# Fixed issue orders around the first experts, and scattered rows read back through slots of the weight ring

## The chip, the cores and the metric

The kernel runs on one core of a Trainium2 chip. The metric is the device time of one execution in microseconds; less is better. The profile is one execution of the same program, with every instruction and every DMA packet recorded. Its engines are PE (matmuls; PEld is the weight load in front of them), DVE (element-wise work), ACT (activations and copies), POOL (small work and indirect DMAs) and SP (a queue that issues DMAs).

## The reference

One transformer layer on 512 tokens of width 1024, in float32: a mixer of three branches (short convolution, sparse attention, gated delta rule), and behind it a hierarchical mixture of experts. The change touches only the second half:

```python
def hier_moe(h, w_rg, b_rg, w_re, b_re, w_eg, w_eu, w_ed):
    ...                               # a group of 4, then 2 of its 8 experts, per token
    order = jnp.argsort(expert)       # tokens sorted by expert
    ...
    def expert_block(args):
        xb, e = args
        return (jax.nn.silu(xb @ w_eg[e]) * (xb @ w_eu[e])) @ w_ed[e]
    ...
    return jax.ops.segment_sum(y, tok_s, num_segments=n_tok).reshape(b, s, dm)
```

There are 32 experts. Each has a gate and an up matrix of 1024x512 and a down matrix of 512x1024, and each of the 512 tokens goes to two experts.

## The kernel before

**Order of work.** The program is traced in Python, and a scheduler then puts each engine's instructions into an order of its own, by the order of the trace and by when it believes their inputs to be there. An engine works through its queue strictly in that order: an instruction that waits holds up all behind it. Two calls add edges. `tc.issue_after(ins)` puts what a block traces on the engine of `ins` behind `ins` in that queue, and does not wait for its end. `tc.keep_in_program_order(ins)` puts one instruction behind the one traced before it on the same engine.

**Experts in pairs.** After the router (L951 to L1007) each expert has 64 slots for tokens. Experts `e` and `e + 16` form a pair, so that there are 16 pairs, and the loop at L1276 runs over them. For each pair the 128 slots' token rows are gathered (`xg`), turned by eight transposes on PE (`pxg`) and scaled on DVE into `xT` (L1109). For each expert of the pair `ffn_up` runs 32 matmuls into `pgu` (L1166, L1167), ACT applies Silu (L1177), DVE multiplies by the up half (L1178), PE turns the result (`pt`, L1184), DVE copies it out as `aT` (L1185), and `ffn_down` runs 16 matmuls into `pd` (L1208).

**Two ways back.** For the pairs in `by_rows` (0, 1, 2, 4, 6, 8, 10) ACT copies `pd` out as `yd`, and POOL scatters its rows by an indirect DMA into `yrows` in DRAM (L1217). For the other pairs the result is split into a high and a low part `y` (L1199 on ACT, L1200 on DVE), DVE makes a 0/1 matrix `sel` from the tokens' numbers `toks` (L1193), and PE multiplies the two into `pc` (L1256), which DVE adds to the output rows `x1p` (L1258). `add_rows` (L1228), called in pairs 12 and 13, works out the row numbers `rix` on POOL, zeroes a tile `yr` for each half of a token tile (L1240), gathers the scattered rows into it (L1241), and has DVE add it to `x1p` (L1245). That is eight `yr` tiles of 128x1024.

**Tables.** The router's results are scattered into eight tables in DRAM, `islots` (L1051), read back into `itab` (L1082), and added up on POOL (L1085, L1086) into `info`. From that POOL makes `tix` (which rows to gather), `yix` (where to scatter), `toks` and `rg` (scales), L1089 to L1101. Pairs 0 and 1 do not need them all: pair 0's rows are picked by matmuls (L1122), and `first_info` (L1132) makes `tix0` for pair 1 and the scales of both.

**Buffers.** The gathered `xg` and the `yr` tiles share one tag of two buffers (`ringa`, tag `raw`). The weights come in chunks of 1 MB through a ring of 18 slots, 12 chunks to a pair, in the order of L1288 and L1290; `wchunk` (L1065) takes the next slot and SP issues the load (L1071), which waits until the slot's last user is done.

```python
    def wchunk(shape, src):
        pool, tag = slots[nslot[0] % len(slots)]
        nslot[0] += 1
        w = pool.tile(shape, F32, tag=tag, name="we")
        ...
            nc.sync.dma_start(w, src)
```

The last expert's down weights come in three pieces, each with its matmuls (L1328), sums and stores.

Of the kernel before, what the change touches and what calls it, by code (L numbers as in the profile page):

```python
# [27 lines left out]
NEXP = 32  # L28
# [71 lines left out]
def kernel(ctx, tc, x, w_in, w_nat, w_small, w_gate, w_branch, w_out, cmp_w1, cmp_w2,  # L100
                       w_rt, consts, params, norm, w_eg, w_eu, w_ed, out, dbg=None):
    nc = tc.nc
    V, A, T, G = nc.vector, nc.scalar, nc.tensor, nc.gpsimd
# [273 lines left out]
    for c in range(NT):  # L377
# [31 lines left out]
        for h in range(4):  # L409
            i = 4 * c + h  # L410
# [609 lines left out]
    b4 = lambda ap, n: ap.unsqueeze(2).to_broadcast([P, NT, n])  # L1020
    V.tensor_tensor(out=ex, in0=ex, in1=mg.to_broadcast([P, NT, 4]), op=ALU.subtract)
    V.tensor_tensor(out=exs[:, :, 4:5], in0=m2, in1=m1, op=ALU.subtract)
    A.activation(exs, exs, AF.Exp)
    A.activation(sc[:, 63:64], mhalf, AF.Silu)
    V.tensor_reduce(out=se, in_=ex, axis=AX.X, op=ALU.add)
    V.scalar_tensor_tensor(out=den, in0=e2, scalar=1.0, in1=se, op0=ALU.add, op1=ALU.mult)
    V.reciprocal(den, den)
# [52 lines left out]
    itab = pair_input().rearrange("p k s -> p (k s)")[:, 0:512].rearrange("p (j c) -> p j c", c=64)  # L1080
    for j, tab in enumerate(islots):
        (nc.scalar if j < 4 else G).dma_start(itab[:, j], tab.rearrange("(p e) c -> p (e c)", p=P))  # L1082
    info = mp.tile([P, NEXP // 2, 4], F32, name="info")
    for n in (4, 2):
        G.tensor_tensor(out=itab[:, 0:n], in0=itab[:, 0:n], in1=itab[:, n:2 * n], op=ALU.add)  # L1085
    G.tensor_tensor(out=info.rearrange("p e c -> p (e c)"), in0=itab[:, 0], in1=itab[:, 1], op=ALU.add)  # L1086

    tix = mp.tile([P, NEXP // 2], I32, name="tix")
    G.tensor_scalar(out=tix, in0=info[:, :, 0], scalar1=4096.0, scalar2=None, op0=ALU.add)  # L1089


    toks, rg = (mp.tile([P, 2, NEXP // 2], F32, name=n) for n in ("toks", "rg"))
    yix = mp.tile([P, 2, NEXP // 2], I32, name="yix")
    for h in range(2):
        hs = slice(64 * h, 64 * h + 64)
        G.tensor_copy(rg[0:64, h], info[hs, :, 1])
        G.tensor_copy(rg[64:128, h], info[hs, :, 2])
        for a in range(2):
            G.tensor_scalar(out=yix[64 * a:64 * a + 64, h], in0=info[hs, :, 3], scalar1=2.0, scalar2=8192.0 + a,
                            op0=ALU.mult, op1=ALU.add)  # L1100
            G.tensor_scalar(out=toks[64 * a:64 * a + 64, h], in0=info[hs, :, 0], scalar1=4096.0, scalar2=None, op0=ALU.add)  # L1101

    def turned(xg):
        xT = pair_input()
# [27 lines left out]
    def first_info():  # L1132
        pi = ps_e.tile([P, 2, 4], F32, tag="pt", name="pi")
        for b in range(2):
            for t in range(NT):
                T.matmul(pi[:, b], row2(t, b), tg[:, t, b], start=t == 0, stop=t == NT - 1)
        V.tensor_copy(info0, pi)
        V.tensor_scalar(out=tix0, in0=info0[:, 1, 0:1], scalar1=4096.0, scalar2=None, op0=ALU.add)
        for h in range(2):
            V.tensor_copy(rg0[0:64, h], info0[64 * h:64 * h + 64, :, 1])  # L1140
            V.tensor_copy(rg0[64:128, h], info0[64 * h:64 * h + 64, :, 2 + h])


    def next_input(pair):
        xg = ringa.tile([P, D], F32, tag="raw", name="xg", bufs=2)
        if pair == 1:
            G.memset(xg, 0.0)
        idx = tix[:, pair:pair + 1] if pair > 1 else tix0
        G.indirect_dma_start(out=xg, out_offset=None, in_=x1rows, in_offset=bass.IndirectOffsetOnAxis(ap=idx, axis=0),
                             bounds_check=S - 1, oob_is_err=False)  # L1150
        inputs.append(turned(xg))

    def slot_info(src, hs):
        gsl = ep.tile([P, 1], F32, tag="gsl", name="gsl", bufs=2)
# [35 lines left out]
    def selection(tok):  # L1190
        sel = lp.tile([P, 512], F32R, tag=("fa", "fb")[nsel[0] % 2], name="sel")
        nsel[0] += 1
        V.tensor_scalar(out=sel, in0=iota, scalar1=tok, scalar2=None, op0=ALU.is_equal)  # L1193
        return sel


# [5 lines left out]
    def ffn_down(aT, wd, tok, between=None, to=None):  # L1202
        pd = mpsum("pd")

        def products(ks):
            for k in ks:
                for a in range(2):
                    T.matmul(pd[64 * a:64 * a + 64], aT[:, k], wd(k, a), start=k == 0, stop=k == 3)  # L1208
                combine_step()

        products((0, 1))
        with tc.issue_after(between()) if between else ExitStack():
            products((2, 3))
        if to is not None:
            y = ep.tile([P, D], F32, tag="y", name="yd", bufs=2)[:, 0:512]
            A.copy(out=y, in_=pd)
            G.indirect_dma_start(out=yrows, out_offset=bass.IndirectOffsetOnAxis(ap=to, axis=0), in_=y, in_offset=None,  # L1217
                                 bounds_check=4 * S - 1, oob_is_err=False)
            return
        y = ep.tile([P, D], F32R, tag="y", name="y", bufs=2)  # L1220
        for a in range(2):
            y_parts(y, halves[a], pd, a)
        rows.append((selection(tok), y))

    by_rows = (0, 1, 2, 4, 6, 8, 10)


    def add_rows(first, last):  # L1228
        if first == 0:
            G.memset(half, 8192.0)  # L1230
            for pair in by_rows:
                G.tensor_scalar(out=psl, in0=at_e, scalar1=float(pair), scalar2=-4096.0, op0=ALU.is_equal, op1=ALU.mult)
                G.tensor_tensor(out=half, in0=half, in1=psl, op=ALU.add)
            G.tensor_tensor(out=half, in0=half, in1=over, op=ALU.add)
            G.tensor_tensor(out=half, in0=half, in1=inf[:, :, :, 3], op=ALU.add)
            G.tensor_copy(rix, half)
        for n in range(first, last):
            t, i = n // 2, n % 2
            yr = ringa.tile([P, D], F32, tag="raw", name="yr", bufs=2)
            G.memset(yr, 0.0)  # L1240
            G.indirect_dma_start(out=yr, out_offset=None, in_=yrows.rearrange("(r a) n -> r (a n)", a=2),  # L1241
                                 in_offset=bass.IndirectOffsetOnAxis(ap=rix[:, t, i:i + 1], axis=0),
                                 bounds_check=2 * S - 1, oob_is_err=False)
            x1 = x1p[t // 2][:, t % 2]
            V.tensor_tensor(out=x1, in0=yr, in1=x1, op=ALU.add)  # L1245

    def combine(pieces=halves):
        todo.extend((tuple(rows), t, cols) for t in range(NT) for cols in pieces)
# [27 lines left out]
    for pair in range(NEXP // 2):  # L1276
# [12 lines left out]
        for h in range(1 if pair == NEXP // 2 - 1 else 2):  # L1289
            ffn_down(up[h][1], weights_down(w_ed[pair + 16 * h]), toks[:, h, pair:pair + 1],  # L1290
                     None if h else up[1][0], yix[:, h, pair:pair + 1] if pair in by_rows else None)
            if h == 0 and len(inputs) == pair + 1 < NEXP // 2:
                next_input(pair + 1)
            if h == 0 and pair in (12, 13):
                add_rows(4 * (pair - 12), 4 * (pair - 11))
        if len(rows) == 2:
            combine()
            rows.clear()
# [146 lines left out]
```

## Time and profile before

| | |
|---|---|
| median of 3 runs | 1226.16 us (1225.51 to 1228.13) |
| the profiled execution's own time | 1225.41 us |
| its span, first to last instruction | 1223.7 us |
| mean granted PE clock | 0.965 of full speed |
| PE busy | 1112.4 us (91%) |
| DVE busy | 555.2 us (45%) |
| ACT busy | 331.7 us (27%) |
| POOL busy | 126.5 us (10%) |
| moved by DMA | 272.42 MB, mean 223 GB/s |

The experts begin about 700 us after the span's start and fill the rest. Busy time of PE is modelled from pipelined matmuls, so that 91% says that PE seldom stands still and not that it runs at its peak. In rows of the timeline the columns are start, duration (both in us), engine, line, operation, output <- inputs, shapes, count, and in brackets how long the engine was idle before and what ended that. A line of the windows gives a stretch, its length, the busy time of PE, PEld, DVE, ACT and POOL with their instructions, and at the end the granted PE clock, the DMA engines' busy share and the rate in GB/s. Line numbers are those of the kernel before.

### The profile page before, as it was taken

To read this page: it belongs to the slowest core of one execution; us is meant where nothing else is said; L and a number is where in the kernel's file an instruction comes from. 1 tells how busy PE (TensorE), PEld (TensorE's weight loads), DVE (VectorE), ACT (ScalarE), POOL (GpSimd) and SP (SyncE) were. 2 spreads that over 40 slices of the span, in tenths; PEclk is the share of its full clock that TensorE was granted. 3 is DMA by queue.
4 is the path that set the end of the run, shared out by engine and by line. 5 is a ranking of instruction groups with operands and counts; after the bars stand their busy time and mean duration, and the time that the engine had idled before them with its cause. 6 is when DMAs were issued, how large, how long until landed. Compare 5 with 4: busy or idle time off the path is not lost.

```text
span 1223.7 us, 15803 instructions
## 1 busy us (share of the span) xinstructions
PE 1112.4 (91%) x6135; PEld 709.6 (58%) x6136; DVE 555.2 (45%) x1258; ACT 331.7 (27%) x644; POOL 126.5 (10%) x210
## 2 busy tenths in 40 slices
PE   0899999999999999999999969997899897997596
PEld 0788798987788887766899524332233333332233
DVE  1677576596444865565353611113041313143435
ACT  2444243343332635565233100110011010110011
POOL 3100211310010000000000341100000000001300
PEclk9999999999999999999999979999899999998799
DMA  8232234212223221100792589999999999999831
GB/s 326 60 101 86 87 94 147 71 52 87 70 71 95 87 86 54 51 2 19 285 376 120 188 322 372 421 420 419 420 420 419 422 420 419 421 420 419 349 137 71
DMA packets 53183, 272.42 MB, mean 223 GB/s; under 512 B 8715, under 2 KB 12683, under 8 KB 28272
## 3 DMA queue, kind: packets, MB, share of 16 engines
q1 hardware_dynamic: 44928, 254.95, 53.7%
q0 software_dynamic: 5600, 12.09, 2.6%
q10 hardware_dynamic: 2576, 4.32, 1.0%
q8 instruction: 50, 0.82, 0.3%
q14 instruction: 29, 0.24, 0.1%
HBM read 267.25 MB, written 12.34 MB: 228 GB/s over the span
## 4 chain that ended last, share of the span: by engine, by line
PE 76%; DMA 12%; issue 6%; DVE 2%; POOL 2%; ACT 1%; POOLq 0%; DVEq 0%; ACTq 0%
PE pgu L1166 9%; PE pmm L189 8%; PE pmm L187 8%; PE pmm L188 8%; PE pd L1208 7%; PE pgu L1167 5%; DMA we<-in_w_eu_dram 3%; PE po L831 3%; PE ptp L825 2%; DMA yr<-yrows,rix 2%; PE pb L188 2%; PE pb L187 2%; PE pb L189 2%; DMA yrows<-zero 2%; DMA we<-in_w_eg_dram 2%
## 5 line engine op out<-in xcount | busy, mean ns | idle before, releaser
L1166 PE MATMUL pgu<-we,xT 128*64 128x512 f32 x512 | 239.8, 615 | 26.4 <-DMA we<-in_w_eg_dram 24.0
L1167 PE MATMUL pgu<-we,xT 128*64 128x512 f32 x512 | 236.4, 608 | 1.4 <-DMA we<-in_w_eu_dram 1.4
L189 PE MATMUL pmm<-hTh,lo 128*128 128x512 f32 x432 | 171.9, 398 | 0.2 <-DVE lo L182 0.2
L187 PE MATMUL pmm<-hTh,hi 128*128 128x512 f32 x432 | 171.1, 396 | 0.0
L188 PE MATMUL pmm<-hTl,hi 128*128 128x512 f32 x432 | 170.7, 395 | 0.0
L182 DVE TENSOR_TENSOR lo<-raw,hi 128x1024 fp32r<-128x1024 f32 x82 | 100.4, 1224 | 114.9 <-ACT hi L181 112.6
L1166 PEld LDWEIGHTS pgu<-we,xT 128*64 128x64 f32 x512 | 68.2, 141 | 126.1 <-issue 117.2
L1208 PE MATMUL pd<-we,aT 128*64 128x512 f32 x496 | 128.4, 622 | 8.8 <-DVE aT L1185 8.8
L181 ACT CAST hi<-raw 128x1024 fp32r<-128x1024 f32 x82 | 86.1, 1050 | 163.9 <-PE pmm L188 94.5
L1177 ACT ACTIVATE act<-pgu,rg 64x512 f32<-64x512 f32 x32 | 21.8, 682 | 272.2 <-PE pgu L1167 182.0
L1167 PEld LDWEIGHTS pgu<-we,xT 128*64 128x64 f32 x512 | 67.2, 140 | 46.3 <-issue 39.4
L189 PEld LDWEIGHTS pmm<-hTh,lo 128*128 128x128 f32 x432 | 81.5, 189 | 17.8 <-DVE lo L182 1.8
L187 PEld LDWEIGHTS pmm<-hTh,hi 128*128 128x128 f32 x432 | 81.7, 189 | 16.6 <-DVE fa L704 0.6
L188 PEld LDWEIGHTS pmm<-hTl,hi 128*128 128x128 f32 x432 | 81.6, 189 | 16.5
L1208 PEld LDWEIGHTS pd<-we,aT 128*64 128x64 f32 x496 | 37.1, 141 | 70.8 <-issue 58.1
L1178 DVE SCALAR_TENSOR_TENSOR act<-pgu,rg,act 64x512 f32<-64x512 f32 x32 | 24.2, 756 | 116.5 <-ACT act L1177 116.1
L1258 DVE TENSOR_TENSOR x<-pc,x 128x512 f32<-128x512 f32 (+2 forms) x76 | 46.9, 658 | 33.2 <-PE pc L1256 32.8
L1185 DVE COPY aT<-pt 128x256 f32<-128x256 f32 x32 | 13.5, 423 | 101.0 <-PE pt L1184 96.9
L1256 PE MATMUL pc<-y,sel 128*128 128x512 f32 (+2 forms) x152 | 50.5, 440 | 8.1 <-DVE y L1200 5.1
L1256 PEld LDWEIGHTS pc<-y,sel 128*128 128x128 f32 x152 | 25.4, 194 | 45.2 <-issue 16.7
L1199 ACT CAST y<-pd 64x512 fp32r<-64x512 f32 (+2 forms) x40 | 21.2, 538 | 105.1 <-PE pd L1208 47.2
L1109 DVE TENSOR_TENSOR xT<-pxg,prm 128x512 f32<-128x512 f32 x32 | 20.9, 684 | 58.3 <-PE pxg L1108 54.7
(796 smaller groups left out, 1786.0 us busy)
## 6 DMA issues: line engine op xcount, KB each, us to landing
we<-in_w_eg_dram SPq DMA_DIRECT2D x64, 1024.0 KB, 20.1
we<-in_w_eu_dram SPq DMA_DIRECT2D x64, 1024.0 KB, 20.1
we<-in_w_ed_dram SPq DMA_DIRECT2D x62, 1024.0 KB, 19.9
raw<-in_w_in_dram SPq DMA_DIRECT2D x30, 512.0 KB, 3.5
raw<-in_w_gate_dram SPq DMA_DIRECT2D x24, 512.0 KB, 3.5
raw<-in_w_branch_dram SPq DMA_DIRECT2D x12, 512.0 KB, 3.5
yrows<-zero POOLq DMA_DIRECT2D x1, 4096.0 KB, 21.7
raw<-in_w_nat_dram SPq DMA_DIRECT2D x8, 512.0 KB, 3.6
```

Source lines behind the costliest of these rows:

```text
L181: A.copy(out=hi, in_=raw)
L182: V.tensor_tensor(out=lo, in0=raw, in1=hi.bitcast(F32), op=ALU.subtract)
L187: T.matmul(ps, ahi(k), bhi(k), start=start and k == 0, stop=False)
L188: T.matmul(ps, ahi(k), blo(k), start=False, stop=False)
L189: T.matmul(ps, alo(k), bhi(k), start=False, stop=stop and k == n - 1)
L825: T.transpose(ptp[:, kt * P:(kt + 1) * P], pts[i][:, kt * P:(kt + 1) * P], ident)
L831: T.matmul(po[64 * hh:64 * hh + 64, qs], nkv[:, kt, 256 + 128 * br + 64 * g:256 + 128 * br + 64 * g + 64], pT[hh][:, kt * P:(kt + 1) * P], ...
L1166: T.matmul(pgu[0:64], xs(k), wg(k), start=k == 0, stop=k == KT - 1)
L1167: ins = T.matmul(pgu[64:128], xs(k), wu(k), start=k == 0, stop=k == KT - 1)
L1208: T.matmul(pd[64 * a:64 * a + 64], aT[:, k], wd(k, a), start=k == 0, stop=k == 3)
L1256: T.matmul(pc[:, 0:n], sel[:, t * P:(t + 1) * P], y[:, cols], start=i == 0, stop=i == len(src) - 1)
L1258: V.tensor_tensor(out=xo, in0=pc[:, 0:n], in1=xo, op=ALU.add)
```

## The change

- The Silu activation of one dummy element (L1024), which loads ACT's table for Silu, is put behind the Exp of the router (L1023) in ACT's queue.
- The gather of pair 1's rows is issued inside `first_info`. The additions of the tables and what follows from them (L1084 to L1101) become a function `tables`, with the same instructions, and are put behind that gather in POOL's queue.
- Each `sel` is put behind the DVE instruction traced before it.
- `add_rows` works on a whole token tile per call: it is called four times instead of twice. The row numbers are worked out behind the last scatter in POOL's queue. Each `yr` is 128x2x1024 and takes a slot of the weights' ring instead of a buffer of `xg`. Its zeroing and its two gathers are put behind the last gather of `xg` traced by then. The DVE additions are still eight of 128x1024.

```diff
-    A.activation(exs, exs, AF.Exp)
-    A.activation(sc[:, 63:64], mhalf, AF.Silu)
+    with tc.issue_after(A.activation(exs, exs, AF.Exp).ins):
+        A.activation(sc[:, 63:64], mhalf, AF.Silu)
...
+    def tables():
+        for n in (4, 2):
+            G.tensor_tensor(out=itab[:, 0:n], in0=itab[:, 0:n], in1=itab[:, n:2 * n], op=ALU.add)
...
             V.tensor_copy(rg0[64:128, h], info0[64 * h:64 * h + 64, :, 2 + h])
-
-
-    def next_input(pair):
+        gathered.append(gather(1))
+        with tc.issue_after(gathered[0][1]):
+            tables()
+
+    gathered = []
+
+
+    def gather(pair):
         xg = ringa.tile([P, D], F32, tag="raw", name="xg", bufs=2)
         if pair == 1:
             G.memset(xg, 0.0)
         idx = tix[:, pair:pair + 1] if pair > 1 else tix0
...
+        return xg, ins.ins
+
+    def next_input(pair):
+        if pair > 1:
+            gathered.append(gather(pair))
+        inputs.append(turned(gathered[-1][0]))
...
-        V.tensor_scalar(out=sel, in0=iota, scalar1=tok, scalar2=None, op0=ALU.is_equal)
+        tc.keep_in_program_order(V.tensor_scalar(out=sel, in0=iota, scalar1=tok, scalar2=None, op0=ALU.is_equal))
...
+            last_scatter.append(ins.ins)
...
-    def add_rows(first, last):
-        if first == 0:
-            G.memset(half, 8192.0)
...
+    def add_rows(t):
+        if t == 0:
+            with tc.issue_after(last_scatter[-1]):
+                G.memset(half, 8192.0)
...
-        for n in range(first, last):
-            t, i = n // 2, n % 2
-            yr = ringa.tile([P, D], F32, tag="raw", name="yr", bufs=2)
+        pool, tag = slots[nslot[0] % len(slots)]
+        nslot[0] += 1
+        yr = pool.tile([P, 2, D], F32, tag=tag, name="yr")
+        with tc.issue_after(gathered[-1][1]):
             G.memset(yr, 0.0)
-            G.indirect_dma_start(out=yr, out_offset=None, in_=yrows.rearrange("(r a) n -> r (a n)", a=2),
...
-            x1 = x1p[t // 2][:, t % 2]
-            V.tensor_tensor(out=x1, in0=yr, in1=x1, op=ALU.add)
+            for i in range(2):
+                G.indirect_dma_start(out=yr[:, i], out_offset=None, in_=yrows.rearrange("(r a) n -> r (a n)", a=2),
...
+        x1 = x1p[t // 2][:, t % 2]
+        for i in range(2):
+            V.tensor_tensor(out=x1, in0=yr[:, i], in1=x1, op=ALU.add)
...
-            if h == 0 and pair in (12, 13):
-                add_rows(4 * (pair - 12), 4 * (pair - 11))
+            if pair in (12, 13):
+                add_rows(2 * (pair - 12) + h)
```

More of the change, by code (lines that the diff above doesn't have):

```diff
@@ L1083 @@
     info = mp.tile([P, NEXP // 2, 4], F32, name="info")
-    for n in (4, 2):
-        G.tensor_tensor(out=itab[:, 0:n], in0=itab[:, 0:n], in1=itab[:, n:2 * n], op=ALU.add)
-    G.tensor_tensor(out=info.rearrange("p e c -> p (e c)"), in0=itab[:, 0], in1=itab[:, 1], op=ALU.add)
     tix = mp.tile([P, NEXP // 2], I32, name="tix")
-    G.tensor_scalar(out=tix, in0=info[:, :, 0], scalar1=4096.0, scalar2=None, op0=ALU.add)
     toks, rg = (mp.tile([P, 2, NEXP // 2], F32, name=n) for n in ("toks", "rg"))
     yix = mp.tile([P, 2, NEXP // 2], I32, name="yix")
[L1094 to L1101, printed above, removed]
+    def tables():
+        for n in (4, 2):
+            G.tensor_tensor(out=itab[:, 0:n], in0=itab[:, 0:n], in1=itab[:, n:2 * n], op=ALU.add)
+        G.tensor_tensor(out=info.rearrange("p e c -> p (e c)"), in0=itab[:, 0], in1=itab[:, 1], op=ALU.add)
+        G.tensor_scalar(out=tix, in0=info[:, :, 0], scalar1=4096.0, scalar2=None, op0=ALU.add)
+        for h in range(2):
+            hs = slice(64 * h, 64 * h + 64)
+            G.tensor_copy(rg[0:64, h], info[hs, :, 1])
+            G.tensor_copy(rg[64:128, h], info[hs, :, 2])
+            for a in range(2):
+                G.tensor_scalar(out=yix[64 * a:64 * a + 64, h], in0=info[hs, :, 3], scalar1=2.0, scalar2=8192.0 + a,
+                                op0=ALU.mult, op1=ALU.add)
+                G.tensor_scalar(out=toks[64 * a:64 * a + 64, h], in0=info[hs, :, 0], scalar1=4096.0, scalar2=None, op0=ALU.add)
     def turned(xg):
@@ L1148, in next_input @@
         idx = tix[:, pair:pair + 1] if pair > 1 else tix0
-        G.indirect_dma_start(out=xg, out_offset=None, in_=x1rows, in_offset=bass.IndirectOffsetOnAxis(ap=idx, axis=0),
-                             bounds_check=S - 1, oob_is_err=False)
-        inputs.append(turned(xg))
+        ins = G.indirect_dma_start(out=xg, out_offset=None, in_=x1rows, in_offset=bass.IndirectOffsetOnAxis(ap=idx, axis=0),
+                                   bounds_check=S - 1, oob_is_err=False)
+        return xg, ins.ins
[3 more added lines that the diff above has]
+        inputs.append(turned(gathered[-1][0]))
     def slot_info(src, hs):
@@ L1216, in ffn_down @@
             A.copy(out=y, in_=pd)
-            G.indirect_dma_start(out=yrows, out_offset=bass.IndirectOffsetOnAxis(ap=to, axis=0), in_=y, in_offset=None,
-                                 bounds_check=4 * S - 1, oob_is_err=False)
+            ins = G.indirect_dma_start(out=yrows, out_offset=bass.IndirectOffsetOnAxis(ap=to, axis=0), in_=y, in_offset=None,
+                                       bounds_check=4 * S - 1, oob_is_err=False)
+            last_scatter.append(ins.ins)
             return
@@ L1225 @@
     by_rows = (0, 1, 2, 4, 6, 8, 10)
-    def add_rows(first, last):
-        if first == 0:
-            G.memset(half, 8192.0)
[L1231 to L1236, printed above, removed]
-        for n in range(first, last):
-            t, i = n // 2, n % 2
-            yr = ringa.tile([P, D], F32, tag="raw", name="yr", bufs=2)
[L1240 to L1243, printed above, removed]
-            x1 = x1p[t // 2][:, t % 2]
-            V.tensor_tensor(out=x1, in0=yr, in1=x1, op=ALU.add)
+    last_scatter = []
@@ new lines, in add_rows @@
+    def add_rows(t):
+        if t == 0:
+            with tc.issue_after(last_scatter[-1]):
+                G.memset(half, 8192.0)
+                for pair in by_rows:
+                    G.tensor_scalar(out=psl, in0=at_e, scalar1=float(pair), scalar2=-4096.0, op0=ALU.is_equal, op1=ALU.mult)
+                    G.tensor_tensor(out=half, in0=half, in1=psl, op=ALU.add)
+                G.tensor_tensor(out=half, in0=half, in1=over, op=ALU.add)
+                G.tensor_tensor(out=half, in0=half, in1=inf[:, :, :, 3], op=ALU.add)
+                G.tensor_copy(rix, half)
+        pool, tag = slots[nslot[0] % len(slots)]
+        nslot[0] += 1
+        yr = pool.tile([P, 2, D], F32, tag=tag, name="yr")
+        with tc.issue_after(gathered[-1][1]):
+            G.memset(yr, 0.0)
+            for i in range(2):
+                G.indirect_dma_start(out=yr[:, i], out_offset=None, in_=yrows.rearrange("(r a) n -> r (a n)", a=2),
+                                     in_offset=bass.IndirectOffsetOnAxis(ap=rix[:, t, i:i + 1], axis=0),
+                                     bounds_check=2 * S - 1, oob_is_err=False)
+        x1 = x1p[t // 2][:, t % 2]
+        for i in range(2):
+            V.tensor_tensor(out=x1, in0=yr[:, i], in1=x1, op=ALU.add)
```

## The prediction

> **What bounds the kernel now.** I read the page for the span, then the windows by stage, then the waits of PE, and at the two places where these show a hole, the timelines of DVE, PE, POOL and SP.
>
> ```profile
> span 1223.7 us, 15803 instructions
> ```
>
> ```profile
> we<-in_w_eg_dram SPq DMA_DIRECT2D x64, 1024.0 KB, 20.1
> ```
>
> ```profile
> 700.00:724.00 24.00, 15.21 (x76) 6.42 (x74) 2.55 (x9) 2.65 (x3) 14.57 (x35) 0.88 0.94 353
> 724.00:740.00 16.00, 13.27 (x46) 4.36 (x44) 2.90 (x5) 1.17 (x2) 4.14 (x9) 0.65 0.62 216
> 740.00:1130.00 390.00, 351.56 (x1543) 131.31 (x1540) 98.29 (x158) 38.20 (x62) 31.78 (x32) 0.95 1.01 418
> 1130.00:1146.00 16.00, 1.41 (x5) 0.71 (x5) 7.83 (x11) 2.22 (x4) 3.81 (x3) 0.50 1.00 414
> 1146.00:1175.00 29.00, 28.83 (x117) 10.82 (x117) 15.28 (x21) 1.36 (x2) 7.75 (x7) 0.96 0.83 312
> 1175.00:1210.00 35.00, 33.47 (x166) 13.44 (x162) 14.93 (x33) 5.66 (x11) 0.00 (x0) 1.00 0.00 0
> ```
>
> ```profile
> PE pgu L1166 <- DMA we<-in_w_eg_dram: 24.0, 4, 10.1
> PE pxg L1108 <- DMA xg<-x1rows,tix: 14.8, 2, 14.6
> PE pd L1208 <- DVE aT L1185: 8.8, 1, 8.8
> ```
>
> From 740 to 1130 the DMA engines are full (share 1.01, 418 GB/s): the weights set the pace, and PE waits for them 24.0 us in four places. A chunk (1024 KB, 1.05 MB) takes 2.5 us at that rate and lands 20.1 us after its issue, so eight are in flight and the ring's other ten slots hold landed chunks. Before 740 the DMA has a hole (0.62), because slots come free late. From 1130 to 1146 PE stands still for a gather, and after 1146 PE is full and the DMA runs dry (0.83, then 0.00): there PE sets the end.
>
> **The front: `sel`, the tables, the second gather.**
>
> ```profile
> 722.60 0.49 DVE L1193 TENSOR_SCALAR sel<-c_moe,toks 128x512 fp32r<-128x512 f32 x1 [10.15 <-POOL toks L1101]
> 723.11 0.42 DVE L1185 COPY aT<-pt 128x256 f32<-128x256 f32 x1
> 728.16 0.49 DVE L1193 TENSOR_SCALAR sel<-c_moe,toks 128x512 fp32r<-128x512 f32 x1 [4.62 <-POOL toks L1101]
> ```
>
> ```profile
> 714.35 0.46 PE L1184 MATMUL pt<-c_ident,act 64*128 64x64 f32 x4
> 723.59 3.68 PE L1208 MATMUL pd<-we,aT 128*64 128x512 f32 x8 [8.79 <-DVE aT L1185]
> 729.58 0.66 PE L1184 MATMUL pt<-c_ident,act 64*128 64x64 f32 x4 [2.31 <-DVE act L1178]
> 730.17 7.92 PE L1208 MATMUL pd<-we,aT 128*64 128x512 f32 x24
> ```
>
> ```profile
> 1081.86 3.65 PE L1208 MATMUL pd<-we,aT 128*64 128x512 f32 x16
> ```
>
> ```profile
> 727.32 0.33 SPq L1071 DMA_DIRECT2D we<-in_w_eg_dram  x1
> ```
>
> Two `sel` stand in DVE's queue at pair 0, which is in `by_rows` and uses none: they belong to pair 3 and wait for `toks`. Behind the first stands `aT` of expert 0, whose input PE had ready at 714.35 + 0.46 = 714.8; behind the second, the act of expert 1, for which PE waits 2.31. PE therefore ends pair 0 at 738.1, 23.3 us after 714.8. At the full clock 32 products at 3.65/16 = 0.23 are 7.3, the copy to `aT` 0.4 and the second turn 0.5, so 723 would do. And the chunk issued at 727.32 waited for the first down slot of pair 0. Pinned behind its own pair's `y`, `sel` waits for nothing here.
>
> What could be late next is pair 1's gather, and the tables.
>
> ```profile
> 717.43 0.72 POOL L1085 TENSOR_TENSOR xT<-xT 128x256 f32<-128x256 f32 x1 [1.71 <-DMA xT<-islots]
> ```
>
> ```profile
> 718.45 1.14 POOL L1149 DMA_INDIRECT xg<-x1rows,tix  x1 [0.16 <-issue]
> ```
>
> ```profile
> xg<-x1rows,tix POOLq DMA_INDIRECT x15, 8.6
> ```
>
> The gather stands behind a table sum that waits for `islots`; POOL was idle for the 1.71 us before it. In front of the sums the gather leaves by 715.7 at the latest and lands 8.6 us later, at 724.3 or before, about when PE wants it (723). Queued behind it on POOL are the sums, which start with their data at 717.4 in either order, and behind them pair 0's scatter and pair 2's gather, which PE wants one pair later: nothing added.
>
> What the front is worth is read from the DMA, since the DMA sets the pace up to 1130: 16 us at 0.62 leave 0.38 x 16 = 6.1 us idle. The 0.06 x 24 = 1.4 us before that are the wait for pair 0's first slot, which does not move. Bounds: 0, if other slots stay late; by rate instead of share 16 x (1 - 216/418) = 7.7. I take **-6.1**, the row that counts the engines' time.
>
> ```profile
> 709.68 1.28 ACT L1177 ACT_TABLE_LOAD   x1 [14.67 <-DMA xT<-islots]
> ```
>
> Silu behind Exp: this load goes from in front of expert 0's act into ACT's idle 14.67 us. The act comes earlier, but PE turns it only at 714.35, behind expert 1's matmuls: 0, at most -1.3.
>
> `sel` later elsewhere: 18 instructions of 0.49. At worst `pc` waits one `sel` in each of nine pairs, 9 x 0.49 = 4.4 us. I take 0, since PE has the next pair's up products to do, or waits for weights.
>
> **The tail: `yr` out of the gathers' buffers.**
>
> ```profile
> 1136.21 1.85 POOL L1149 DMA_INDIRECT xg<-x1rows,tix  x1 [10.95 <-DVE x L1245]
> ```
>
> ```profile
> 1085.44 2.84 PE L1256 MATMUL pc<-y,sel 128*128 128x512 f32 x10
> ...
> 1105.38 1.97 PE L1166 MATMUL pgu<-we,xT 128*64 128x512 f32 x2 [3.33 <-DMA we<-in_w_eg_dram]
> ```
>
> ```profile
> 1124.26 1.20 PE L1256 MATMUL pc<-y,sel 128*128 128x512 f32 x4
> ...
> 1145.49 1.94 PE L1108 MATMUL pxg<-c_ident,xg 128*128 128x128 f32 x8 [14.59 <-DMA xg<-x1rows,tix]
> 1147.08 1.20 PE L1256 MATMUL pc<-y,sel 128*128 128x512 f32 x2
> 1148.21 0.70 PE L1166 MATMUL pgu<-we,xT 128*64 128x512 f32 x1
> ```
>
> Pair 14's gather waits for DVE to free one of the two buffers that it shares with `yr`; it leaves at 1136.21, and PE, which had ended its `pc` before that, gets it at 1145.49. With `yr` elsewhere the gather waits only for pair 12's `xg` to be turned, two pairs earlier. PE loses 1148.21 - 1125.46 = 22.75 us, in which it also does 8 `pc` (2.3 us at the 0.284 of the ten quoted) and 8 transposes (1.9): 18.5 lost. Lower bound the bare wait, 14.6. After it PE is full to the end (28.83 of 29, 33.47 of 35), so what PE gains there the kernel gains: **-18.5**. Cover: pair 14's twelve chunks, issued from 1090.08 on (quoted below) 2.5 apart, have landed by 1090 + 28 + 20 = 1138, the down weights last, which PE wants only behind both experts' up products. The weights do not hold up the rest: they are all there by 1175, or 1170 without the DMA's idle 0.17 x 29, and the 35 us of full PE work behind 1175 need none.
>
> The halved clock is in that number: 0.50 from 1130 to 1146. The Trainium skill ("TensorE: Matmul & The Clock Gate", part 1) says that PE falls to half rate after an idle window of about 3.4 us and needs about as long at work to come back; the granted clock agrees. By that rule the term would be an estimated 14.6 + 1.7 = 16.3.
>
> The eight gathers of `yr` now go early.
>
> ```profile
> 1061.23 1.03 POOL L1241 DMA_INDIRECT yr<-yrows,rix  x1 [6.59 <-DMA yrows<-yd,yix]
> ```
>
> ```profile
> 1090.76 1.02 POOL L1241 DMA_INDIRECT yr<-yrows,rix  x1 [0.28 <-POOL yr L1240]
> ```
>
> ```profile
> q0 software_dynamic: 1520, 2.60, 4.0%
> ```
>
> ```profile
> yr<-yrows,rix POOLq DMA_INDIRECT x8, 8.2
> ```
>
> From 1040 on, the queue q0 of the view of DMA moves 2.60 MB in 11 indirect DMAs, 0.24 MB each. These two were issued before PE's last wait for weights (1105.38), six later; now all eight are before it. Six more, 1.4 MB at 418 GB/s, are 3.4 us in front of weights that set the pace; upper bound, whole tiles of 512 KB, 7.5; lower 0, if they fall behind that wait after all. **+3.4**. The Trainium skill's rule that DMAs from SP, ACT and POOL share the same 16 engines and interleave ("Trainium Kernel Development and Optimization", key constraints) speaks for a price; the rows agree, 8.2 us for a gather in the midst of 20 us chunks.
>
> Four `yr` also take four turns of the ring: the look-ahead falls from 18 to 15 or 16 chunks for about two pairs. Eight in flight fill the DMA, so seven remain landed or in use: 0. SP is in order, so a `yr` that is held late would stop it (a rival below). The row numbers, some 18 POOL operations of 0.2 us, lie beside the 6.59 us wait for the last scatter's landing: 0. Zeroing is the same area in half as many pieces; the eight DVE sums are the same.
>
> Sum: -6.1 - 18.5 + 3.4 = **-21.2**. The profiled execution took 1225.4 (span 1223.7), so 1204.2; the median of the runs shown lies 0.8 higher: **1205**, span 1202.5.
>
> **The rivals.**
>
> *The front gain is eaten in the middle.* The gathers cost 7.5 and the front gives little, or PE, 90% busy there, has too little slack to follow. Then only the tail counts: -14.6 to -18.5 with +0 to +4, about 1211. For it: the last wait for weights is only 3.3 us long. Against: there are four, 24.0 us in all, the last as late as 1105.
>
> *The ring is held.*
>
> ```profile
> 1119.52 2.49 DVE L1245 TENSOR_TENSOR x<-yr,x 128x1024 f32<-128x1024 f32 x2
> ```
>
> ```profile
> 1090.08 0.33 SPq L1071 DMA_DIRECT2D we<-in_w_eg_dram  x1
> ```
>
> The first two `yr` were summed at 1119.52, though the first had been gathered by 1061 + 8 = 1069. The first `yr`'s slot goes to pair 14's first chunk, issued at 1090.08. If DVE's order stays so late, SP stops for 29 us, of which 20.1 are covered by chunks in flight: +9, about 1214. Against: the two tiles were summed together, the second waited for the shared buffers, and that is gone.
>
> *The gather of pair 14 stays late.* POOL's order is the scheduler's, and nothing puts that gather ahead of the first two `yr`. If a `yr` there still waits for a late event, only -6.1 + 3.4 remains: 1223.
>
> *The other side: DVE stops at the sums.*
>
> ```profile
> 1155.53 1.23 DVE L1245 TENSOR_TENSOR x<-yr,x 128x1024 f32<-128x1024 f32 x1 [5.38 <-DMA yr<-yrows,rix]
> ```
>
> If the scheduler takes a gather to be landed when it is only issued, DVE waits up to 8.2 us at each of four tiles, with `aT` and `act` behind it, in a stretch where PE has 3.3 us to spare: 4 x 8.2 - 3.3 = 29.5, against 21.2 that makes 1234. It decides from some 6 us a tile on (4 x 6 - 3.3 = 20.7). Against: one of eight sums waited so long before.
>
> **How the numbers follow.** Main case 0.66; middle 0.14; ring 0.06; late gather 0.06; DVE 0.08. Main case alone: -7.7 - 18.5 + 0 = -26.2 gives 1200, and -3 - 14.6 + 3.4 = -14.2 gives 1212. To leave out no more than 2 in 10 the range takes in the middle and the ring, with some 4 us on each side for an order that the scheduler changes elsewhere: 1196 to 1218. Within 0.2% of before (2.5 us, what a measurement of this kernel can tell from no change) lies most of the late gather: same 0.05. Slower is the DVE case but for its milder part: 0.07. Faster 0.88.
>
> **What would show it.** Right: no `sel` in DVE's queue before pair 3; `pd` of pair 0 from about 715; the DMA share between 724 and 740 near 1; pair 14's gather issued well before 1100, and no wait of PE for `xg` above 1 us; PE without a hole from 1100 to the end; the last weights landing under 10 us earlier, and PE's last product some 21 us earlier. Wrong: PE waits for `xg` or weights after 1100, SP held by DVE's sums, DVE waiting for `yr`, or an order of PE in the middle that has changed by itself.

## The result, and the profile after

| | before | after |
|---|---|---|
| median of the runs, us | 1227.1 (1225.5 to 1228.1) | 1195.8 (1194.4 to 1196.3) |
| ratio, 95% interval | 1 | 0.9745 (0.9728 to 0.9761) |
| profiled execution: time, span, mean granted clock | 1225.4, 1223.7, 0.965 | 1194.4, 1192.7, 0.981 |

The gain is 31 us where 21 were forecast; the median lies 0.2 us under the range. The direction and the two places were right, the size was not, and most of the experiments below are about the other 10 us.

The windows by stage of the kernel after; the columns are PE, PEld, DVE, ACT and POOL busy, then the granted clock, the DMA share and GB/s:

```profile
span 1192.7 us, 15823 instructions
```

```profile
700.00:724.00 24.00, 23.35 (x118) 9.53 (x114) 3.85 (x11) 2.54 (x4) 13.72 (x28) 1.00 0.93 352
724.00:740.00 16.00, 15.71 (x78) 7.11 (x80) 2.59 (x5) 1.36 (x2) 2.30 (x3) 1.00 1.02 417
740.00:1130.00 390.00, 345.58 (x1530) 127.97 (x1528) 113.32 (x177) 39.04 (x64) 43.55 (x54) 0.96 1.01 419
1130.00:1146.00 16.00, 16.00 (x77) 6.91 (x74) 8.69 (x14) 2.52 (x4) 0.00 (x0) 1.00 1.00 414
1146.00:1175.00 29.00, 25.91 (x126) 9.89 (x123) 11.93 (x27) 3.32 (x6) 0.00 (x0) 1.00 0.47 178
```

Both holes are gone: 724 to 740 has 417 GB/s (216 before), and PE works 16.00 of 16 between 1130 and 1146 (1.41 before). Among PE's waits the one for `xg` is no longer there; the weights lead the list, with 31.5 us after 700 where they had 25.4:

```profile
PE pgu L1177 <- DMA we<-in_w_eg_dram: 24.6, 5, 11.2
PE pgu L1178 <- DMA we<-in_w_eu_dram: 6.9, 6, 1.7
```

The front, from the timelines of DVE, POOL and PE (`aT` is line 1196 now, the gather 1155, `pd` 1219):

```profile
714.66 0.42 DVE L1196 COPY aT<-pt 128x256 f32<-128x256 f32 x1 [3.67 <-PE pt L1195]
...
717.51 0.42 DVE L1196 COPY aT<-pt 128x256 f32<-128x256 f32 x1 [1.38 <-PE pt L1195]
```

```profile
710.98 1.08 POOL L1155 DMA_INDIRECT xg<-x1rows,tix  x1 [0.39 <-DVE act L1189]
```

```profile
715.14 1.94 PE L1219 MATMUL pd<-we,aT 128*64 128x512 f32 x8 [0.52 <-DVE aT L1196]
...
722.70 1.16 PE L1109 MATMUL pxg<-c_ident,xg 128*128 128x128 f32 x8
```

No `sel` stands there, the down products begin at 715.1 and pair 1's turning at 722.7, as forecast (715 and 723). The tail, from the timelines of POOL and PE:

```profile
1024.07 1.02 POOL L1155 DMA_INDIRECT xg<-x1rows,tix  x1 [3.07 <-PE pxg L1109]
...
1073.68 1.10 POOL L1258 DMA_INDIRECT yr<-yrows,rix  x1 [0.16 <-POOL yr L1256]
...
1082.87 0.99 POOL L1258 DMA_INDIRECT yr<-yrows,rix  x1 [0.30 <-issue]
```

```profile
1113.67 0.94 PE L1274 MATMUL pc<-y,sel 128*128 128x512 f32 x3 [0.77 <-ACT y L1210]
1116.60 0.64 PE L1177 MATMUL pgu<-we,xT 128*64 128x512 f32 x1 [2.00 <-DMA we<-in_w_eg_dram]
```

Pair 14's gather leaves at 1024 instead of 1136, all eight gathers of `yr` within 10 us, and pair 14 begins at 1116.60 instead of 1148.21. That is 31.6 us, the whole gain: from there to the end both kernels need about the same, 76.1 us now and 75.5 before.

### The profile page after: what moved, and what is told of

Read it like the earlier page. It is cut to its first block, busy times and chain, and to the rows that moved or that the text cites. A ratio compares the mean times of both kernels' runs of the same rounds, so it can differ in the third digit from the quotient of the medians.

```text
span 1192.7 us, 15823 instructions
## 1 busy us (share of the span) xinstructions
PE 1097.3 (92%) x6135; PEld 705.9 (59%) x6136; DVE 556.0 (47%) x1258; ACT 328.9 (28%) x642; POOL 124.2 (10%) x206
## 4 chain that ended last, share of the span: by engine, by line
PE 68%; DMA 28%; DVE 2%; ACT 1%; POOL 1%; issue 0%; SPq 0%; POOLq 0%; ACTq 0%; DVEq 0%
DMA we<-in_w_eu_dram 16%; PE pmm L189 8%; PE pmm L187 8%; PE pmm L188 8%; DMA we<-in_w_ed_dram 8%; PE pgu L1178 5%; PE pgu L1177 4%; PE po L831 3%; PE pd L1219 3%; PE ptp L825 2%; PE pb L188 2%; PE pb L187 2%; DMA we<-in_w_eg_dram 2%; PE pb L189 2%; DMA yrows<-zero 2%; PE pmn L556 1%
## 5 line engine op out<-in xcount | busy, mean ns | idle before, releaser
L182 DVE TENSOR_TENSOR lo<-raw,hi 128x1024 fp32r<-128x1024 f32 x82 | 100.6, 1227 | 116.0 <-ACT hi L181 114.7
L1219 PE MATMUL pd<-we,aT 128*64 128x512 f32 x496 | 121.9, 598 | 5.6 <-DVE y L1211 4.0
L1188 ACT ACTIVATE act<-pgu,rg 64x512 f32<-64x512 f32 x32 | 21.8, 681 | 294.4 <-PE pgu L1178 192.1
L189 PEld LDWEIGHTS pmm<-hTh,lo 128*128 128x128 f32 x432 | 81.5, 189 | 17.9 <-DVE lo L182 1.8
L1274 PE MATMUL pc<-y,sel 128*128 128x512 f32 (+2 forms) x152 | 44.4, 417 | 2.3 <-DVE x L1276 1.4
L1210 ACT CAST y<-pd 64x512 fp32r<-64x512 f32 (+2 forms) x40 | 21.2, 538 | 86.9 <-PE pd L1219 41.3
L187 PE MATMUL pb<-yhi,hi 128*128 128x512 f32 x96 | 37.7, 398 | 1.3 <-ACT yhi L536 1.3
```

The source lines that it names most:

```text
L182: V.tensor_tensor(out=lo, in0=raw, in1=hi.bitcast(F32), op=ALU.subtract)
L187: T.matmul(ps, ahi(k), bhi(k), start=start and k == 0, stop=False)
L189: T.matmul(ps, alo(k), bhi(k), start=False, stop=stop and k == n - 1)
L1274: T.matmul(pc[:, 0:n], sel[:, t * P:(t + 1) * P], y[:, cols], start=i == 0, stop=i == len(src) - 1)
```

## The experiments

Chunks are named by pair, expert (A or B), weight (g, u, d) and half: 13Bg0 is the first gate chunk of pair 13's second expert. A pin is an added edge of order between two instructions of one queue. A line number in a row is that of its own kernel.

| run | what it is | us | ratio, 95% interval |
|---|---|---|---|
| e6 | slots alone | 1209.7 | 0.9846 (0.9830 to 0.9861) |
| e5 | row numbers' pin alone | 1217.4 | 0.9906 (0.9888 to 0.9925) |
| e2 | slots and row numbers (the whole of `add_rows`) | 1198.2 | 0.9767 (0.9751 to 0.9783) |
| e1 | the front's three pins alone | 1208.3 | 0.9846 (0.9829 to 0.9862) |
| e15 | of these, the selections | 1209.2 | 0.9854 (0.9827 to 0.9882) |
| e16 | of these, the tables | 1222.3 | 0.9955 (0.9942 to 0.9969) |
| e13 | front's pins and slots | 1199.4 | 0.9772 (0.9744 to 0.9799) |
| e14 | front's pins and row numbers | 1213.9 | 0.9889 (0.9861 to 0.9917) |
| e4, e9 | before, SP in program order: everywhere; from pair 13 | 1229.9, 1224.1 | 1.0011, 0.9969 |
| e3 | after, SP in program order everywhere | 1210.8 | 0.9864 (0.9847 to 0.9880) |
| e7 | after, pair 13 in the old order, 14 and 15 in program order | 1207.9 | 0.9833 (0.9816 to 0.9851) |
| e12, e17 | after, pairs 13 to 15 in program order; with other slots | 1195.7, 1196.7 | 0.9732, 0.9756 |
| e8, e18 | after, pairs 14 and 15 in program order; with other slots | **1187.8, 1187.3** | 0.9671 (0.9657 to 0.9685), 0.9680 |
| e10, e11 | e8 without the gathers of `yr`; with each twice | 1190.2, 1205.5 | 0.9693, 0.9810 |

Differences below are taken between ratios, times 1227 us; each side is known to about 2 us, in e13 to e15 to some 3.5.

### Which edit gives what

**e1**, the front's pins; `add_rows` as before:

```diff
...
-        yr = pool.tile([P, 2, D], F32, tag=tag, name="yr")
+            yr = ringa.tile([P, D], F32, tag="raw", name="yr", bufs=2)
...
```

> The changed kernel with the reading back of the scattered rows as it was before (yr in the gathers' two buffers, four gathers at pair 12 and four at pair 13); the pinned selections, the tables behind the second gather and Silu behind Exp stay. Theory 'by rate': the DMA's hole at 724 to 740 is to be counted in bytes, the weights run 9.7 us earlier from there on, and pair 14's gather still comes late: 1216 to 1218 us, pair 14 starting at about 1138. Theory 'by share' (the prediction's term): 6.1, 1220. Theory 'order': the pinned selections also turn the order in which SP issues pair 13's last up chunks and its down chunks, and that alone is worth up to 9 us of PE's time in pair 13: then 1208 to 1212. All three expect PE to wait for pair 14's xg by over 10 us.

**e2**, `add_rows` of the kernel after in the kernel before (the inverse edit).

> The kernel before with only the scattered rows read back through ring slots (and their pins). Theory 'two things and an order': the front's 9.7 us are missing, and so is SP's turned order at pair 13; PE ends pair 13's down products at about 1128 (the gathers' cost of 3 to 6 us on top of before) and begins pair 14 some 4 us later: 1209 to 1213 us, 14 to 17 below the kernel before. Theory 'the two parts add up': the changed kernel's 31.3 less 9.7, so 1205 to 1206. The prediction's terms: -18.5 + 3.4, so 1211.

**e5**, the row numbers' pin alone, in the kernel before:

```diff
+            with tc.issue_after(last_scatter[-1]):
                 G.memset(half, 8192.0)
...
```

> The kernel before with one edit alone: the 18 POOL operations that make the row numbers are pinned behind the last scatter; yr stays in the gathers' buffers, selections and tables are as before. Theory 'row numbers': these operations, which stand on POOL between 712 and 718 in the kernel before, are what keeps the second gather and toks late, so the front's whole 9 to 10 us come from this edit: pair 1 begins at about 724 instead of 739.6, the weights run 10 us earlier, pair 13 keeps its old order of chunks and pair 14's gather comes about 10 us earlier with DVE's sums: 1216 to 1218 us. Rival (the prediction, which costed these operations at nothing): 1225 to 1228, pair 1 beginning at 739.

**e6**, e2 without that pin.

> The kernel before with yr in ring slots and pinned behind the last input gather, but with the row numbers left where the scheduler puts them. Theory 'row numbers': the front stays as in the kernel before (pair 1 beginning at about 739), and only the tail is won, 18 to 21 us: 1205 to 1209. Rival: the slots alone shift the scheduler's whole order, and the front comes with them: 1198, as with both.

e2 alone gave 28.6 of the 31.3 us, the front's part among them, though it touches nothing in the front's code. The windows by stage of e6, e2 and e5, in this order:

```profile
724.00:740.00 16.00, 12.84 (x41) 4.17 (x42) 2.58 (x5) 1.10 (x2) 3.87 (x10) 0.60 0.61 214
```

```profile
724.00:740.00 16.00, 15.77 (x78) 7.12 (x80) 2.56 (x5) 1.36 (x2) 3.13 (x4) 1.00 1.02 418
```

```profile
724.00:740.00 16.00, 15.57 (x79) 7.06 (x80) 2.59 (x5) 1.36 (x2) 2.88 (x3) 1.00 1.02 419
```

Of these three, the two that pin the row numbers late have the DMA's hole at 724 filled; in e6, where they are free, it stays. The timeline of POOL in the kernel before shows why (the first and the last of 13 of the 18 operations, which stand there), and that of DVE in e2 what follows:

```profile
712.17 0.24 POOL L1232 TENSOR_SCALAR psl<-slt 128x8 f32<-128x8 f32 x1
...
718.10 0.19 POOL L1236 CAST rix<-slt 128x8 int32<-128x8 f32 x1
```

```profile
717.45 0.42 DVE L1188 COPY aT<-pt 128x256 f32<-128x256 f32 x1 [1.37 <-PE pt L1187]
720.43 0.52 DVE L1196 TENSOR_SCALAR sel<-c_moe,toks 128x512 fp32r<-128x512 f32 x1 [2.56 <-POOL toks L1101]
```

The row numbers stood ahead of the second gather and of `toks`. Without them the scheduler puts both `sel` behind both `aT` by itself. So e5 is worth 11.5 us, e6 18.9, together 30.4, and e2 has 28.6: for these two, the parts add up.

**e13**, the kernel after without the row numbers' pin; **e14**, the kernel after with `yr` in the gathers' buffers; **e15**, the kernel before with `tc.keep_in_program_order(...)` around `sel` alone; **e16**, the kernel before with `gathered.append(gather(1))` and `tables()` behind it alone.

> The changed kernel without one pin: the 18 POOL operations of the row numbers go where the scheduler puts them (they stand in front of the second gather again). Theory 'either is enough': with the selections out of DVE's way the front is whole without moving the row numbers, 1195 to 1199 us. Rival 'the row numbers are the front': pair 1 begins at 739 again and the time is 1204 to 1207.

> The kernel before with the front's pins and the row numbers' pin, yr still in the gathers' buffers (the changed kernel without the slots). Theory 'either is enough': the two front edits do not add up, so as the front's pins alone, 1206 to 1209 us, pair 14's gather at about 1111. Rival 'they add up': 1197 to 1200.

> The kernel before with the selections pinned and nothing else. Theory (the prediction's reading of the front): the two selections in DVE's queue were what held pair 0, so the front is won and SP's order at pair 13 is turned with it: 1207 to 1211 us, as with all three pins, pair 1 beginning at 726 to 728 (its gather still stands behind a table sum). Rival: the gather's place is what counts, then 1220 or more.

> The kernel before with the tables pinned behind the second gather and nothing else. Theory (the prediction's reading): the selections still stand ahead of pair 0's turned input on DVE and wait for toks until 722 to 728, so nothing is won: 1225 to 1228.5 us. Rival: the earlier gather alone starts pair 1 earlier: 1215 to 1222.

On top of the slots, either front edit gives nearly the same: 9.7 us for the row numbers (e6 to e2), 9.1 for the pins (e6 to e13); the second adds 2.7 to 3.3, which these intervals don't tell from nothing. One thing on record would fit it: in e2 PE still waits 3.44 us for a gate chunk in the middle of pair 13, and in the kernel after it does not; no run shows this wait alone.

```profile
1094.17 1.12 PE L1169 MATMUL pgu<-we,xT 128*64 128x512 f32 x1 [3.44 <-DMA we<-in_w_eg_dram]
```

Of the pins the selections do the work (e15). The tables alone leave both `sel` where they were (722.6 and 728.0) and give 5.5, more than the nothing that was expected: expert 1's `act` now stands ahead of the second `sel`, and pair 1's turning comes at 732.8 instead of 738.0.

But e1 and e15 gave 18.9 and 17.9, twice the front's share. POOL and DVE in e1 show that the pins also moved the tail:

```profile
1111.00 0.99 POOL L1155 DMA_INDIRECT xg<-x1rows,tix  x1 [7.60 <-DVE x L1259]
```

```profile
1087.08 1.22 DVE L1259 TENSOR_TENSOR x<-yr,x 128x1024 f32<-128x1024 f32 x1
```

DVE's first sum of `yr` comes at 1087 instead of 1119.5, a buffer is free earlier, and pair 14's gather leaves at 1111 instead of 1136 (at 1112 in e15, with the selections alone pinned). The time of e1 lies in the range of the theory "order", but by another path: PE waits 3.5 us for pair 14's `xg` there, where all three theories had over 10. In e5 that chain only moves with the rest: the gather leaves at 1125.9 and PE's wait is as long as ever.

```profile
1135.52 1.95 PE L1108 MATMUL pxg<-c_ident,xg 128*128 128x128 f32 x8 [14.91 <-DMA xg<-x1rows,tix]
```

So e1's second half lies where the slots also gain, and is not counted twice. e14, with the row numbers added to e1, came out slower than e1, not the same as expected: its second sum stands at 1106.3 instead of 1099.9, and its gather leaves at 1117.4. Why the scheduler moves that sum is open.

### The order in which SP loads the chunks

With the selections pinned, the scheduler also issues pair 13's up chunks ahead of its down chunks; in the kernel before 13Bg0 and 13Bu0 stood behind all four. The theory after the first comparison was that this order made the missing 10 us.

```diff
-            nc.sync.dma_start(w, src)
+            tc.keep_in_program_order(nc.sync.dma_start(w, src))     # e3 (after), e4 (before): all chunks
```

> The changed kernel with all chunks of the weights issued by SP in program order (each pair's eight up chunks ahead of its four down chunks). Theory 'order': pair 13 already has that order in the changed kernel, so its time hardly moves: 1193 to 1198 us. Rival: the scheduler's mixed order keeps SP from waiting for slots, and without it the stream stops: 1201 or more, with a lower DMA rate between 740 and 1100.

> The kernel before with all chunks of the weights issued by SP in program order, nothing else. Theory 'order': PE no longer waits 3.3 us at pair 13's last up chunks, its second act comes about 9 us earlier than 1117.0, and with it DVE's sums and pair 14's gather: 1216 to 1219 us. Rival 'absorbed': PE is earlier in pair 13 but the gather of pair 14 is not, the hole only grows: 1225 to 1228.

Both kernels were spoilt by something else: the pin puts the very first chunks behind everything that SP issued until then. In e3 the whole stream comes 16 us later (its 139th chunk, the rows of SP in the kernel after and in e3), and the time by 14.6:

```profile
1002.33 0.33 SPq L1071 DMA_DIRECT2D we<-in_w_eu_dram  x1
```

```profile
1017.91 0.33 SPq L1071 DMA_DIRECT2D we<-in_w_eg_dram  x1
```

In e4 that chunk is 6 us later than in the kernel before, and the time is 1.3 us longer, which its interval (0.9996 to 1.0025) does not tell from nothing: before the change the tail waited for its gather (14.6 us, and 14.9 in e4), not for the stream. The next kernels force the order for the last pairs only, from a list:

```diff
+    chunk_order = {13: "Ag0 Au0 Bg1 Bu1 Ad0 Ag1 Au1 Ad1 Bd0 Bd1 Bg0 Bu0",                # e7; e9, e12: program order
+                   14: "Ag0 Au0 Ag1 Au1 Bg0 Bu0 Bg1 Bu1 Ad0 Ad1 Bd0 Bd1",                # e8 has 14 and 15 alone
+                   15: "Ag0 Au0 Ag1 Au1 Bg0 Bu0 Bg1 Bu1 Ad0 Ad1"}
```

> The changed kernel with SP's order of chunks forced for pairs 13 to 15: pair 13 as in the kernel before (the first two chunks of its second expert behind all four down chunks), pairs 14 and 15 in program order. To be read against the run with pairs 14 and 15 in program order alone. Theory 'order': PE waits over 2 us for the second expert of pair 13 again, its act comes some 9 us later than 1102.4, and pair 14 begins 5 to 9 us later: 1199 to 1204 us. Rival 'order is worth nothing': within 2 us of the other run.

> The changed kernel with SP's order forced for pairs 14 and 15 alone: program order, so that the first gate chunk of pair 14, which the scheduler puts fifth (issued at 1094.1, PE waits 2.0 us for it at 1116.6), goes first. Theory 'pair 14 starts with that chunk, and behind it PE is the bound': the wait goes, 1193.5 to 1195 us. Rival: another chunk of pair 14 is as late, or PE's half clock moves elsewhere: 1195.5 to 1197.

> The kernel before with SP's order of chunks forced for pairs 13 to 15: program order, so that pair 13's second expert has its up chunks ahead of the down chunks; nothing else. Theory 'order': the second act of pair 13 comes 5 to 10 us earlier than 1117.0, DVE's sums of yr and with them pair 14's gather follow: 1216 to 1221 us. That would also explain why the pinned selections alone, which turn this order as a by-product, gave 19 us and not 10. Rival: the gather's chain does not follow PE, the hole only grows: 1225 to 1229.

> The changed kernel with SP's order forced to program order for pair 13 too, not for 14 and 15 alone. Theory 'order counts where the first chunk that PE wants is not first': pair 13's first chunk is first already in both, so 1186.5 to 1189 us, as with 14 and 15 alone. Rival: the scheduler's mixed order in pair 13 is the better one: 1190 or more.

In the kernel before, program order from pair 13 on is worth 3.8 us (e9), less than the 6 to 11 expected, and PE's wait for the gather stays at 14.9. In the kernel after, the old order of pair 13 costs 20 against e8 (e7), with PE waiting 3.5 and 2.1 us for the chunks of 13B; in e7 the ring is disturbed too, so the 20 are no clean price of the order. e12 differs from e7 in that order alone and in the slots that follow from it, and there it costs 12.4.

e8 gave 8 us more than the change by the medians, 9.1 by the ratios, where 2 were expected. In the kernel after SP issues 14Ag0, the first chunk that PE wants of pair 14, fifth. With eight chunks in flight, a chunk's landing shows as the issue of the eighth behind it, and that one is at 1116.62, where PE's wait ends at 1116.60. The two rows of SP:

```profile
1094.11 0.33 SPq L1071 DMA_DIRECT2D we<-in_w_eg_dram  x1
...
1116.62 0.33 SPq L1071 DMA_DIRECT2D we<-in_w_eg_dram  x1
```

In e8 14Ag0 goes first; the timeline of PE and the window:

```profile
1109.00 1.02 PE L1181 MATMUL pgu<-we,xT 128*64 128x512 f32 x2
```

```profile
1100.00:1130.00 30.00, 30.00 (x136) 14.51 (x136) 17.39 (x25) 3.99 (x7) 0.00 (x0) 1.00 1.01 419
```

Pair 14 begins at 1109.0, beside pair 13's last down products, at a clock of 1.00. The same window of the kernel after:

```profile
1100.00:1130.00 30.00, 26.69 (x113) 10.21 (x113) 16.31 (x23) 3.01 (x5) 0.00 (x0) 0.94 1.01 420
```

Seeing only the 2.0 us of the wait left out that PE's order changes with it. e8 fixes the order of all chunks of pairs 14 and 15, so that the gain is not shown to come from that one chunk.

e12, with pair 13 in program order too, gives 7.5 back. In it SP stands still, which looked like the rival "the ring is held":

```profile
1072.73 8.14 SPq L1073 DMA_DIRECT2D we<-in_w_ed_dram  x4
1103.39 0.33 SPq L1073 DMA_DIRECT2D we<-in_w_eg_dram  x1
```

The chunk at 1103.39 takes the slot of the first `yr`, whose second sum ends at 1102.11 + 1.22. e17 and e18 give that slot to a chunk that is loaded last:

```diff
+                for n in "Bd1 Ag0 Au0 Bd0 Ag1 Au1 Bg0 Bu0 Bg1 Bu1 Ad0 Ad1".split():   # slots of pair 14, in the ring's order
```

> The kernel with pairs 13 to 15 in program order (1195.7 us), with one more edit: the slots that the first two yr tiles held go to the two chunks of pair 14 that are loaded last, not to its first chunk. The weights, their order on SP and all else are the same. Theory 'the ring is held': the 22 us in which SP stands still there (1080.9 to 1103.4, until DVE has summed the first yr) go, pair 14's first chunk lands before PE wants it: 1187 to 1191 us. Rival: PE waits there for DVE (its sel and the sums), not for weights, and the time stays: 1194.5 to 1197.

> The fastest kernel so far (pairs 14 and 15 in program order, 1187.8 us) with the same edit of the slots. SP stands still for 9.5 us there (until 1089.6). Theory: PE waits for no weight after 1100 in it, so the time does not move: 1186.5 to 1189 us. Rival: the stream's earlier chunks let the scheduler's order of PE gain more: 1183 to 1186.

SP's stop is gone in e17, and the time is the same:

```profile
1082.83 0.33 SPq L1077 DMA_DIRECT2D we<-in_w_eg_dram  x1
```

The theory of the held ring falls. What e17 shares with e12 and not with e8 is the order on DVE (e17, then e8):

```profile
1097.10 0.76 DVE L1197 SCALAR_TENSOR_TENSOR act<-pgu,rg,act 64x512 f32<-64x512 f32 x1 [10.01 <-ACT act L1196]
1097.88 1.23 DVE L1271 TENSOR_TENSOR x<-yr,x 128x1024 f32<-128x1024 f32 x1
```

```profile
1087.07 3.61 DVE L1267 TENSOR_TENSOR x<-yr,x 128x1024 f32<-128x1024 f32 x3
```

In e8 four sums use the time before pair 13's first act; in e17 they stand behind it, DVE idles 10.0 us, and then eight sums lie between 1098 and 1123 among the work that PE wants (PE waits 5.5 us for `sel` there). That fits, but no run moved the sums alone.

### What the gathers cost

```diff
-            for i in range(2):
-                G.indirect_dma_start(out=yr[:, i], ...)       # left out of e8's kernel in e10; in e11 the two lines stand twice
```

> The changed kernel with pairs 14 and 15 in program order (the fastest so far, 1187.8 us), and without the eight indirect DMAs that gather the scattered rows: yr is zeroed and summed as before, the rows of seven pairs are not read back. What the gathers cost. The prediction's term (1.4 MB and more in front of weights that set the pace): 3 to 6 us faster, 1182 to 1185. Theory 'they delay the stream by 6 us, but PE no longer waits for a weight after them': 1187 to 1188.5, though chunk 178 is issued 5 to 6 us earlier.

> The same kernel with each of the eight gathers issued twice (the same rows into the same place). The prediction's term: 3 to 6 us slower than 1187.8. Theory 'slack': the stream has some 2 to 5 us left at pair 14, so 0 to 4 slower; beyond that a wait for pair 14's first chunk, or DVE waiting for the later landing (about 1125 instead of 1105), shows in PE.

The first chunk of pair 15, rows of SP in e8 and e10:

```profile
1117.11 0.33 SPq L1073 DMA_DIRECT2D we<-in_w_eg_dram  x1
```

```profile
1111.91 0.33 SPq L1073 DMA_DIRECT2D we<-in_w_eg_dram  x1
```

Without the gathers that chunk is issued 5.2 us earlier. Of these, 1.2 stand there before the first gather (the 161st chunk of each), so that the eight gathers delay the stream by 4.0; their 1.9 MB at 418 GB/s would be 4.5.

```profile
1060.59 0.33 SPq L1073 DMA_DIRECT2D we<-in_w_eg_dram  x1
```

```profile
1059.43 0.33 SPq L1073 DMA_DIRECT2D we<-in_w_eg_dram  x1
```

The time is not shorter (0.9693 against 0.9671), but that is no clean price: without the gathers the scheduler also puts DVE's sums earlier, and PE waits for the DVE work behind them. Between 1060 and 1100 PE works 34.5 of 40 us in e10 at a clock of 0.96, and 37.7 at 1.00 in e8.

```profile
1083.46 0.71 PE L1113 MATMUL pxg<-c_ident,xg 128*128 128x128 f32 x4 [2.15 <-DVE x L1276]
```

So e10 does not show that the gathers cost nothing; their price stays open. Twice as many cost 17 us, more than either theory said, and PE waits only 1.4 us for a weight there. DVE waits for a landing with `aT` behind the sum, the rival "DVE stops at the sums", and SP waits for the slots:

```profile
1106.76 1.22 DVE L1271 TENSOR_TENSOR x<-yr,x 128x1024 f32<-128x1024 f32 x1 [7.36 <-DMA yr<-yrows,rix]
```

```profile
1108.49 3.68 PE L1223 MATMUL pd<-we,aT 128*64 128x512 f32 x8 [5.93 <-DVE aT L1200]
```

```profile
1100.00:1130.00 30.00, 21.07 (x86) 8.25 (x83) 19.14 (x25) 2.90 (x5) 3.96 (x4) 0.89 0.82 317
```

## Why the prediction was right in its places, and where its steps failed

The sum was -6.1 - 18.5 + 3.4 = -21.2. The path e6, e2, after gives -18.9, -9.7 and -2.7. The places and the direction held. Three steps failed: the front's term was too small, the row numbers' was put at nothing, and the gathers' price was charged to a wait that went away.

- **Front, -6.1 against 9.1 to 9.7: the term was mis-sized by the measure.** The hole was counted by the DMA's busy share, 0.38 x 16, and only up to 740. Counted in bytes it was 7.7, the bound that stood beside it, and it did not end at 740: up to 752 the kernel before moved 353 GB/s, and 12 x (1 - 353/419) = 1.9. 7.7 + 1.9 = 9.6, and the 139th chunk is issued 9.65 us earlier (at 1002.33, shown above, and before at 1011.98). The share overstated the rate in both stretches: 0.62 where 216/418 is 0.52, and 0.97 where 353/419 is 0.84. The rows of the kernel before:

```profile
740.00:752.00 12.00, 12.00 (x58) 5.00 (x56) 0.82 (x2) 0.68 (x1) 1.51 (x2) 1.00 0.97 353
752.00:800.00 48.00, 46.40 (x232) 18.70 (x230) 9.02 (x15) 4.49 (x7) 5.10 (x5) 1.00 1.01 419
```

```profile
1011.98 2.45 SPq L1071 DMA_DIRECT2D we<-in_w_ed_dram  x2
```

- **The row numbers, "lie beside the 6.59 us wait for the last scatter: 0": the step failed.** That is where they go, not where they came from. They stood at 712 to 718 ahead of the second gather and of `toks`; taking them away is worth 11.5 us alone. The prediction gave the front to the selections. They suffice (e15), but so do the row numbers; both were in the change and either was enough. That this error does not show in the sum is luck.
- **The tail, -18.5: not contradicted.** Slots are worth 18.9 alone, 17.1 on top of e5 and 17.7 on top of e14, with the gathers' price in each; on top of e1, whose pins had already moved the gather, they are worth 9.1. By the rule of the Trainium skill ("TensorE: Matmul & The Clock Gate", part 1) the term would have been an estimated 16.3. Two of the first three lie nearer to 18.5 and one nearer to 16.3, and these runs do not tell the two apart.
- **The eight early gathers, +3.4: the size fits the stream, the path failed.** All eight delay the stream by some 4.0 us, where the term counted six of them. But the term was charged to PE's wait at 1105.38, for 13Bg0, which the new order of SP had moved ahead of the gathers; the only wait for a weight that PE has behind them is the 2.0 us at 14Ag0. What they cost in the end stays open, since e10 is no clean price.
- **What is left of the 10 us** (9.7 - 6.1 = 3.6 for the front, 18.9 - 15.1 = 3.8 for the tail) is the 2.7 us of the second front edit on top. It may be chance, or the 3.44 us wait of e2.
- **The signs.** `sel`, `pd` at 715, the DMA's hole, pair 14's gather and PE's wait for `xg` came as named. "PE without a hole" holds but for some 3 us in 1100 to 1130 and again in 1146 to 1175. "The last weights under 10 us earlier" was wrong: the last down chunk is issued at 1151.3 instead of 1168.0, since PE, 31 us earlier, gives the slots back earlier.
- Costed at nothing: the look-ahead of the ring (e17, e18: rightly), `sel` later elsewhere (no wait of PE for `sel` among the waits after 700 in the kernel after), Silu (not tried alone).
- The rivals: none decided. "DVE stops at the sums" showed only with each gather issued twice (e11). "An order of PE in the middle that has changed by itself" was the sign named for a miss; orders that changed by themselves are what e1, e8 and e12 turned up.

## What to carry to other kernels

Read a hole in a DMA-bound stretch in GB/s against the full stretch, not in busy share, and in stretches short enough to show where the rate is full again. Where a scheduler makes the queues, an instruction that is pinned somewhere moves others far away: ask of each moved operation what it stood in front of, and list the order of the queues before and after, by tile. After a fix, look at which load the first product waits for: an order of the last two pairs' chunks that puts that load first was worth another 8 to 9 us. And when a run takes work out to price it, check that the other queues kept their order.

## What was not expected of the hardware

An indirect gather of 0.24 MB landed 8.2 us after its issue (the median before, when the gathers of `yr` were spread out among the weights); of eight issued within 10 us, the last landed 21.8 us after its issue, at 1104.7 (1082.87 + 21.8). In e8, where all eight landings are on record, the first took 8.6 us and the last 21.7, so that they landed some 3.2 us apart. And a stream that came 15.6 us later (e3) lengthened the time nearly in full, by 14.6, while one that came 6.3 us later in the kernel before (e4) changed it by nothing that can be measured.
